# One ring of raw weight tiles for all stages, and a post-norm whose steps are tied to chunks

## The chip, the cores and the metric

The kernel runs on one core of one Trainium2 chip. The metric is the device time of one execution in microseconds (us), the median over the runs. Every time below is in us unless marked ns.

## The reference

The kernel computes two layers of a decoder trunk on 1024 tokens of width 1024, all in float32. Cut to what matters:

```python
for l in range(2):
    h = rms_norm(x, pre_mix_norm[l])
    z = h @ w_in[l]                     # conv columns, q, k, v of 4 heads
    u = silu(layer_norm(dwconv31(c_a * sigmoid(c_g))))
    o = (softmax(q1 k1^T) - lam * softmax(q2 k2^T)) v    # causal, rotary on part of q and k
    m = concat([u, rms_norm(o) * c]) @ w_out[l]
    x = x + rms_norm(m, post_mix_norm[l])
    h = rms_norm(x, pre_ffn_norm[l])
    g, val = split(dwconv3(h @ w_up[l]))                 # 2 x 2816 columns
    f = (gelu(g) * val) @ w_down[l]
    x = x + rms_norm(f, post_ffn_norm[l])
```

## The kernel before

Each layer is two stages, each with tile pools of its own in SBUF. The mixing stage holds both projections, the convolution and the attention. The feed-forward stage holds the up-projection (with the short convolution and the gate) and the down-projection.

Every matrix product is made to float32 accuracy from rounded parts. A weight block comes from memory as a "raw" tile. ScalarE (ACT) copies it to a rounded high part; VectorE (DVE) or GpSimd (POOL) subtracts to get the low part; TensorE (PE) then runs three matmuls for each pair of blocks. In the mixing stage this is the helper pair `load` (L443) and `split` (L458): raw tile `raw` of 512 columns in a ring of RAW = 3 in pool `mw`, parts in `whw`, `wlw`, `whq`, `wlq`. In the feed-forward stage it is `parts` (L1276), with the parts in `wo` (seven buffers) and, in the down-projection, `wp` (five buffers).

The mixing stage is ordered by a planner, `Flow`. It keeps a clock for each engine and emits instructions in the order in which its costs say they become ready. Its `Ring` objects mirror the numbers of buffers, RAW among them, so that another RAW gives another plan. It orders PE, DVE, ACT and POOL.

The up-projection uses a Strassen-like scheme of seven products for each pair of column tiles, written out as a list `seq` of slots; `prep` (L1396) splits one weight operand, seven slots ahead. Its raw weight tiles are 1024 columns wide (512 KB), in two tags, `rg` and `rv`, of two buffers each, in the stage's pool `fw_`. `next_raw` (L1379) starts one load; it is called four times ahead of the first slot and then after certain splits. The first eight columns named in EARLY run ahead as products "e1" and "e2".

The down-projection runs seven products j = 1, 2, 5, 3, 6, 7, 4, each over K2 = 11 chunks k (`run`, L1613). In each chunk it prepares the operands of the chunk that comes three later, and the last two or three chunks are a tail in which PE finishes one token tile after the other. After product 6 the first half of the tokens is complete but for a sum that the function `end6` makes; its post-norm, and in the first layer the next layer's pre-norm and transposes, are a generator for each of four token tiles, `post_steps(tt)`. A queue `bg` of the four is stepped two or three times in each chunk, so that two generators are under way together:

```python
def step(q):
    g = q.popleft()
    if next(g, None) is not None:
        q.insert(min(1, len(q)), g)
```

Each generator takes one tile `y` and one tile `xr`, both from rings of two. `end7` makes the other half's sum from the PSUM banks, `pa`, that product 4 goes on to accumulate in; `end4` is the second half's post-norm.

The order of the DMA queue (SP, shown as SPq) isn't written by hand: the framework places each load where it becomes ready by its own schedule, in any order of the program. A tile in a pool that is open for the whole program needs a free slot for that; a tile in a stage's pool needs in addition the pool to have opened, after what came before in that part of SBUF. `gvec` loads the norm gains into a ring of two in such a lasting pool: the calls that bear on this are L1603, near the end of the up-projection, and L1745, late in the down-projection, for the next layer.

Of the kernel before, what the change touches and what calls it, by code (L numbers as in the profile page):

```python
# [9 lines left out]
F32 = mybir.dt.float32  # L10
# [7 lines left out]
P = 128  # L18
# [3 lines left out]
HB = 512  # L22
# [33 lines left out]
E_BUFS = 5  # L56
LATE = 12
XR = 2
RAW = 3
AT_BUFS = 2  # L60
CB = ((9, 0, 1, 2), (0, 1, 2, 3))

# [151 lines left out]
def build(tc, ap, out):  # L214
# [7 lines left out]
    with ExitStack() as top:  # L222
# [9 lines left out]
        ptr = pool(top, "ptr", bufs=2, space=PSUM)  # L232
        pO = pool(top, "pO", bufs=1, space=PSUM)
        dr = pool(top, "dr", bufs=1, space=DRAM)

        def const(name, shape, dt=F32):
            return cst.tile(shape, dt, tag=name, name=name)
# [178 lines left out]
        for l in range(DEPTH):  # L416
            xres = xin if l == 0 else x2[l - 1]
            with ExitStack() as st:
# [24 lines left out]
                def load(key, src, n, tag, gate=None):  # L443

                    wi = yield from R[tag].get()
                    size, bufs = (768, 4) if tag == "q" else (1024, 2)
                    hi = mw.tile([P, size], F32R, tag=f"wh{tag}", name=f"wh{tag}", bufs=bufs)
                    lo = mw.tile([P, size], F32R, tag=f"wl{tag}", name=f"wl{tag}", bufs=bufs)
                    W[key] = hi, lo, wi
                    step = n if n <= HB else n // 2  # L450
                    for j in range(n // step):
                        ri = yield from R["raw"].get()
                        raw = mw.tile([P, HB], F32, tag="raw", name="raw", bufs=RAW)
                        s = slice(j * step, (j + 1) * step)
                        sy.dma_start(raw[:, :step], src[:, s])
                        fl.spawn(split(key, j, raw[:, :step], hi[:, s], lo[:, s], step, ri, gate), fl.now + W_LAT)
# [809 lines left out]
            with ExitStack() as st:  # L1266
# [36 lines left out]
                with ExitStack() as su:  # L1303
# [64 lines left out]
                    for tt in range(4):  # L1368
                        before[NORM_T[tt]] = tt
                        for step in range(4):  # L1370
# [2 lines left out]

                    raws, wsum, W = {}, {}, {}

                    loads = deque([("e", n, "gv"[q % 2], 0) for q, n in enumerate(early)]
                                  + [("m", n, "gv"[v], v) for n in range(NFT) for v in range(2)])

                    def next_raw():  # L1379
                        if loads:  # L1380
                            k, n, t, v = loads.popleft()
                            raw = fw_.tile([P, 1024], F32, tag="r" + t, name="raw", bufs=2)
                            sy.dma_start(raw, wu[2 * order[n] + v])
                            raws["gv"[v], (k, n)] = raw[:, 0:HB], raw[:, HB:1024]

# [10 lines left out]
                    def prep(j, n):  # L1396
                        g = raws["g", ("e" if j in ("e1", "e2") else "m", n)]
                        if j in (6, 5, 7, 3):
                            if j == 6:
                                wsums(n, 1, 2)  # L1400
                            elif j in (5, 7):
                                wsums(n, 3 if j == 5 else 4)
                            x = wsum[n][{6: 2, 5: 1, 7: 3, 3: 4}[j]]
                        elif j == 4:
                            x = raws["v", ("m", n)][1]
                        else:
                            x = g[j in (2, "e2")]
                        W[j, n] = parts(x, po)
                        if j in ("e2", 3, 4):
                            next_raw()  # L1410

                    for _ in range(4):
# [197 lines left out]
                with ExitStack() as sd:  # L1610
                    dn = pool(sd, f"dn{l}", bufs=1, reuse_waits="tile")

                    def run(j, ps, first, tail, ends):  # L1613

                        c0 = [x[0] for x in chunks].index(j)
                        cuts = [(k,) for k in range(K2 - tail)] + [tuple(range(K2 - tail, K2))]
                        for cut in cuts:
                            for k in cut:
                                c = c0 + k
                                for _ in range(1 + c % 2):  # L1620
                                    fetch()
                                for ahead, task in ((F_AHEAD, fetch_f), (P_AHEAD, prepare)):
                                    if c + ahead < len(chunks):
                                        task(c + ahead)
                                sum_w(c)
                                for _ in range(2 + (j == 7 and k % 2)):
                                    if bg:
                                        step(bg)
                            for tt in range(4):
                                ts = slice(tt * P, (tt + 1) * P)  # L1630
                                for k in cut:
                                    (ah, al), (wh, wl) = ops[c0 + k]
                                    for n, (x, y) in enumerate(((ah[:, ts], wh), (al[:, ts], wh), (ah[:, ts], wl))):
                                        pe.matmul(ps[tt], x, y, start=first and k + n == 0, stop=k == K2 - 1 and n == 2,  # L1634
                                                  skip_group_check=not first)
                                if cut[-1] == K2 - 1 and j == 4:
                                    ends(tt)
                        if j != 4:
                            for tt in range(4):
                                ends(tt)  # L1640

                    bg = deque()

                    def step(q):

                        g = q.popleft()
                        if next(g, None) is not None:
                            q.insert(min(1, len(q)), g)

                    def post_steps(tt):  # L1650

                        m0, s2 = m0s[tt]
                        ps1 = u2[tt]
                        y = xs.tile([P, YW], F32, tag="y", name="y", bufs=2)[:, 0:D]
                        xr = load_x(x1[l][tt])
                        se.activation(y[:, 0:HB], ps1, AF.Square, accum_out=s2[:, 1:2])
                        ve.tensor_tensor(y[:, HB:D], ps1, g_pf[:, HB:D], op=ALU.mult)
                        ss = xs.tile([P, 1], F32, tag="ss", name="ss", bufs=3)
                        ve.tensor_tensor(ss, s2[:, 0:1], s2[:, 1:2], op=ALU.add)
                        r = rstd_from_sum(ss, 1.0 / D)  # L1660
                        yield 1
                        ve.scalar_tensor_tensor(y[:, 0:HB], m0, r, xr[:, 0:HB], op0=ALU.mult, op1=ALU.add)  # L1662
                        ve.scalar_tensor_tensor(y[:, HB:D], y[:, HB:D], r, xr[:, HB:D], op0=ALU.mult, op1=ALU.add)  # L1663
                        sy.dma_start(out[tt * P:(tt + 1) * P, :] if last else x2[l][tt], y)
                        if last:
                            return
                        ss = xs.tile([P, 1], F32, tag="ss", name="ss", bufs=3)
                        se.activation(xr, y, AF.Square, accum_out=ss)
                        yield 1
                        r = rstd_from_sum(ss, 1.0 / D)  # L1670
                        yield 1
                        ve.scalar_tensor_tensor(xr, y, r, g_pre, op0=ALU.mult, op1=ALU.mult)
                        yield 1
                        yield 1
                        sl = slice(tt * P, (tt + 1) * P)
                        for gi in range(2):
                            pt = ptr.tile([P, 4, P], F32, tag="tr", name="pt")
                            for j in range(4):
                                pe.transpose(pt[:, j, :], xr[:, (gi * 4 + j) * P:(gi * 4 + j + 1) * P], ident)
                            se.activation(nhA[gi][:, 0, :, sl], pt, AF.Copy)  # L1680
                            yield 1
                            ve.tensor_tensor(nhA[gi][:, 1, :, sl], pt, f32(nhA[gi][:, 0, :, sl]), op=ALU.subtract)
                            yield 1

                    def keep(name):
                        return [dn.tile([P, HB], F32, tag=name, name=name, bufs=4) for _ in range(4)]
# [9 lines left out]
                    own = [dn.tile([P, HB], F32, tag="wb", name="wb", bufs=12) for _ in range(12)]  # L1696
                    spB = [t[:, j] for t in inB for j in range(8)]
                    B.update({"dn": dn, "12": spB[0:K2], "22": own[1:12], "21": B["A"][K2:16] + spB[K2:16] + own[0:1]})
                    pa = banks(0)
                    u2, vv = keep("u2"), keep("vv")  # L1700
                    for _ in range(5):
# [42 lines left out]
                    else:  # L1744
                        g_pre = gvec(l + 1, 0)  # L1745
                        nhA = alloc_h("hA")
                    bg.extend(post_steps(tt) for tt in range(4))
                    run(7, pa, False, DTAIL, end7)

                    def end_last(tt):  # L1750
                        nonlocal nhB
                        if tt == 0:
                            while bg:
                                step(bg)
                            manual.close()
                            if not last:
                                nhB = alloc_h("hB")
# [75 lines left out]
```

## Time and profile before

| | |
|---|---|
| time, median of 3 runs | 2364.84 |
| lowest and highest | 2364.63, 2525.17 |
| profiled execution | 2363.12 |
| its span, first to last instruction | 2361.0 |
| mean granted TensorE clock | 0.969 of full speed |
| weight data and all else moved by DMA | 295.39 MB |

The profile is of one execution. PE is matmuls, PEld weight loads, which overlap them; DVE, ACT, POOL and SP are the other engines. A row of the chain of waits says which line of the program waited for which, and how long. In the timeline a bracket gives the idle time of that engine ahead of the instruction and what ended it. L1634 are the matmuls of the down-projection, L1583 those of the up-projection, L495 those of the mixing stage; L1279 is ACT's half of a split, L1280 the subtraction. In the first layer the mixing stage takes the first 500, and the down-projection ends near 1190.

### The profile page before, as it was taken

Reading aid. Unit: us, or ns where it says so; the run is one execution under the profiler, and the core shown is the slowest. Engines: PE = TensorE matmul, PEld = TensorE weight load, DVE = VectorE, ACT = ScalarE, POOL = GpSimd, SP = SyncE. Lnnn points to the kernel's source line nnn. Section 1 sums busy time; section 2 is a strip of 40 time slices with the busy share of each in tenths; the row PEclk is TensorE's granted clock in tenths of the full one; section 3 lists DMA queues with packets and bytes.
Section 4 is the critical chain, followed back from the end, with each engine's and each line's share of the span. In section 5 each row is a group of like instructions: output and inputs, shape, how many; then the busy total and the mean of one; then the engine's idle time right before and its main releaser. Section 6 shows DMA issues by size and latency. Waiting matters only on the chain. (4 is left out here: it accounts for less than half of the span.)

```text
span 2361.0 us, 31535 instructions
## 1 busy us (share of the span) xinstructions
PE 2203.4 (93%) x10568; PEld 1837.9 (78%) x10568; DVE 1857.8 (79%) x3285; ACT 1131.9 (48%) x2458; POOL 827.4 (35%) x896
## 2 busy tenths in 40 slices
PE   6999997959999999999879999979699999999997
PEld 4998886748877878788659988867588778787886
DVE  6889989537888888777768899895478888887777
ACT  4445456535544544444534455565364444445443
POOL 3224312235454554201532233122345445542024
PEclk8999998979999999999979999989899999999999
DMA  4222323534333333933333133235443333348343
GB/s 145 69 63 90 85 80 111 188 137 161 107 125 118 123 130 114 321 110 93 126 114 81 52 89 90 75 112 196 144 143 107 125 128 111 132 138 310 101 151 108
DMA packets 140129, 295.39 MB, mean 125 GB/s; under 512 B 16832, under 2 KB 33984, under 8 KB 139456
## 3 DMA queue, kind: packets, MB, share of 16 engines
q1 hardware_dynamic: 139968, 293.39, 38.9%
q8 instruction: 83, 1.36, 0.2%
q14 instruction: 78, 0.64, 0.1%
HBM read 198.44 MB, written 78.12 MB: 117 GB/s over the span
## 5 line engine op out<-in xcount | busy, mean ns | idle before, releaser
L1634 PE MATMUL pd<-wp,wo 128*128 128x512 f32 x1776 | 409.8, 392 | 8.3 <-DVE wp L1280 4.9
L1634 PEld LDWEIGHTS pd<-wp,wo 128*128 128x128 f32 x1776 | 333.7, 189 | 81.2 <-DVE wp L1280 6.5
L1583 PE MATMUL py<-t,wo 128*128 128x512 f32 x1584 | 377.4, 391 | 4.5 <-DVE cg L1451 4.5
L1583 PEld LDWEIGHTS py<-t,wo 128*128 128x128 f32 x1584 | 296.6, 188 | 73.3 <-ACT wo L1279 7.7
L1280 POOL TENSOR_TENSOR wo<-ws,wo 128x512 fp32r<-128x512 f32 x176 | 252.8, 1448 | 283.0 <-ACT wo L1279 251.2
L1583 PE MATMUL px<-hA,wo 128*128 128x512 f32 x1056 | 262.6, 401 | 43.3 <-ACT wo L1279 42.1
L1583 PEld LDWEIGHTS px<-hA,wo 128*128 128x128 f32 x1056 | 200.3, 190 | 93.5 <-ACT wo L1279 43.0
L1280 POOL TENSOR_TENSOR wo<-raw,wo 128x512 fp32r<-128x512 f32 x132 | 176.7, 1343 | 146.3 <-ACT wo L1279 136.9
L1280 POOL TENSOR_TENSOR wo<-fa,wo 128x512 fp32r<-128x512 f32 x66 | 102.4, 1568 | 311.2 <-ACT wo L1279 287.0
L1279 ACT ACTIVATE wo<-ws 128x512 fp32r<-128x512 f32 x176 | 108.4, 626 | 135.3 <-PE py L1583 54.5
L1469 DVE SCALAR_TENSOR_TENSOR acc<-cg,fw,acc 128x512 f32<-128x512 f32 x176 | 132.6, 753 | 41.7 <-ACT acc L1457 38.0
L593 DVE SCALAR_TENSOR_TENSOR scr<-u,cw,scr 128x256 f32<-128x256 f32 (+2 forms) x288 | 159.7, 574 | 0.3
L495 PE MATMUL pq<-whq,hA 128*128 128x384 f32 x512 | 136.4, 348 | 5.9 <-ACT whq L459 5.9
L1457 ACT ACTIVATE acc<-cg,fb,fw 128x512 f32<-128x512 f32 x88 | 68.2, 775 | 147.8 <-DVE cg L1451 147.8
L495 PE MATMUL pq<-whq,hB 128*128 128x384 f32 x512 | 134.4, 343 | 0.0
L1583 PE MATMUL pz<-b,wo 128*128 128x512 f32 x528 | 131.1, 397 | 2.0 <-DVE cv L1451 2.0
L1583 PE MATMUL pz<-t,wo 128*128 128x512 f32 x528 | 130.5, 396 | 0.0
L848 ACT ACTIVATE e<-S,mxv 128x512 f32<-128x512 f32 (+2 forms) x192 | 109.7, 578 | 42.4 <-DVE mxv L843 30.9
L853 POOL TENSOR_TENSOR sm<-sm 128x1 f32<-128x1 f32 x64 | 29.5, 461 | 274.6 <-ACT e L848 274.6
L839 DVE TENSOR_REDUCE mxv<-S 128x1 f32<-128x512 f32 (+2 forms) x192 | 100.6, 548 | 28.3 <-PE S L823 26.2
L1583 PEld LDWEIGHTS pz<-b,wo 128*128 128x128 f32 x528 | 98.4, 188 | 28.2 <-issue 5.2
L1583 PEld LDWEIGHTS pz<-t,wo 128*128 128x128 f32 x528 | 99.0, 188 | 23.6
(279 smaller groups left out, 4985.3 us busy)
## 6 DMA issues: line engine op xcount, KB each, us to landing
raw<-in_wupd SPq DMA_DIRECT2D x104, 512.0 KB, 3.7
fa<-f SPq DMA_DIRECT2D x154, 256.0 KB, 2.7
f<-fs SPq DMA_DIRECT2D x88, 256.0 KB, 3.6
raw<-in_wmix SPq DMA_DIRECT2D x80, 256.0 KB, 2.9
f<-gg SPq DMA_DIRECT2D x66, 256.0 KB, 2.0
raw<-in_wmix SPq DMA_DIRECT2D x64, 192.0 KB, 2.5
qs<-sth SPq DMA_DIRECT2D x64, 128.0 KB, 2.8
os<-onT SPq DMA_DIRECT2D x16, 512.0 KB, 2.9
```

Source lines behind the costliest of these rows:

```text
L495: mm = pe.matmul(dst, a, b, start=first and k + j == 0, stop=final and k == n - 1 and j == 2)
L593: ve.scalar_tensor_tensor(dst, src, wk, dst, op0=ALU.mult, op1=ALU.add)
L839: ve.tensor_reduce(mv_[:, j:j + 1], S, axis=AX.X, op=ALU.max, negate=True)
L848: se.activation(e[:, c0:c0 + w], S, AF.Exp, bias=mv_[:, 0:1], accum_out=sm[:, j:j + 1])
L853: po.tensor_tensor(sm[:, 0:1], sm[:, 0:1], sm[:, 1:2], op=ALU.add)
L1279: se.activation(w[:, 0], raw, AF.Copy)
L1280: eng.tensor_tensor(w[:, 1], raw, f32(w[:, 0]), op=ALU.subtract)
L1457: se.activation(acc[n, v, hf], C[n][v][:, 2 + hf * HB:2 + hf * HB + HB], AF.Identity, bias=fb[:, mt:mt + 1], scale=fw[:, mt, 2:3])
L1469: ve.scalar_tensor_tensor(dst, c[:, j + hf * HB:j + hf * HB + HB], fw[:, mt, j:j + 1], a, op0=ALU.mult, op1=ALU.add)
L1583: pe.matmul(ps, x, y, start=first and k + j == 0, stop=k == 3 and j == 2, skip_group_check=not first)
L1634: pe.matmul(ps[tt], x, y, start=first and k + n == 0, stop=k == K2 - 1 and n == 2, skip_group_check=not first)
```

## The change

A pool `rw` is opened at the start of the program and stays open. The raw tiles of both stages come from it: one tag, RAW = 4 buffers of 1024 columns. The mixing stage's ring so grows from three to four, in the plan too, and the up-projection's two tags become one ring in the same order of loads. One of the calls of `next_raw` moves from behind the split for product 3 to behind that for product 7, one slot earlier in `seq`.

The queue `bg` becomes a list, and each generator advances by at most one step in a chunk: tile 0 from chunk 0 of product 7, tile 1 from chunk 3, tile 2 from chunk 6, tile 3 from chunk 8, and all in every chunk of product 4. The steps are cut anew: the square and the first product are a step of their own, and the last subtraction no longer has one.

```diff
-RAW = 3
+RAW = 4
+        rw = pool(top, "rw", bufs=1)
...
-                        raw = mw.tile([P, HB], F32, tag="raw", name="raw", bufs=RAW)
+                        raw = rw.tile([P, 1024], F32, tag="raw", name="raw", bufs=RAW)
...
-                    loads = deque([("e", n, "gv"[q % 2], 0) for q, n in enumerate(early)]
-                                  + [("m", n, "gv"[v], v) for n in range(NFT) for v in range(2)])
+                    loads = deque([("e", n, 0) for n in early] + [("m", n, v) for n in range(NFT) for v in range(2)])
...
-                            raw = fw_.tile([P, 1024], F32, tag="r" + t, name="raw", bufs=2)
+                            k, n, v = loads.popleft()
+                            raw = rw.tile([P, 1024], F32, tag="raw", name="raw", bufs=RAW)
...
-                        if j in ("e2", 3, 4):
+                        if j in ("e2", 7, 4):
                             next_raw()
...
-                                for _ in range(2 + (j == 7 and k % 2)):
-                                    if bg:
-                                        step(bg)
+                                for tt, q in enumerate((0, 3, 6, 8)):
+                                    if j == 7 and k >= q or j == 4:
+                                        next(bg[tt], None)
...
                         ve.tensor_tensor(y[:, HB:D], ps1, g_pf[:, HB:D], op=ALU.mult)
+                        yield 1
                         ss = xs.tile([P, 1], F32, tag="ss", name="ss", bufs=3)
...
                             ve.tensor_tensor(nhA[gi][:, 1, :, sl], pt, f32(nhA[gi][:, 0, :, sl]), op=ALU.subtract)
-                            yield 1
...
-                    bg.extend(post_steps(tt) for tt in range(4))
+                    bg = [post_steps(tt) for tt in range(4)]
                     run(7, pa, False, DTAIL, end7)
...
-                            while bg:
-                                step(bg)
+                            for g in bg:
+                                for _ in g:
+                                    pass
```

## Rows read from the trace of the kernel before

**Rows 1.** The page, part 1: busy time, share of the span, instructions.

```profile
...
PE 2203.4 (93%) x10568; PEld 1837.9 (78%) x10568; DVE 1857.8 (79%) x3285; ACT 1131.9 (48%) x2458; POOL 827.4 (35%) x896
```

**Rows 2.** TensorE's waits, whole span: us in total, times, longest us.

```profile
...
PE px L1583 <- ACT wo L1279: 42.1, 2, 23.1
...
PE pg L495 <- ACT whw L459: 9.3, 1, 9.3
...
PE pq L495 <- ACT whq L459: 5.9, 4, 4.1
...
PE pt L1679 <- DVE xr L1672: 5.2, 3, 2.1
```

**Rows 3.** Timeline, first layer's mixing end: start, us, engine, line [idle before].

```profile
...
508.15 0.58 ACT L1156 ACTIVATE pw<-pw 128x512 f32<-128x512 f32 x1 [4.51 <-DVE xn L1153]
...
512.40 0.18 ACT L1172 ACTIVATION_READ_ACCUMULATOR xn<-xe 128x1 f32 x1
...
514.80 0.33 SPq L246 DMA_DIRECT2D gb<-in_norms  x1
...
516.34 10.78 SPq L1383 DMA_DIRECT2D raw<-in_wupd  x6
520.99 0.63 ACT L1279 ACTIVATE wo<-raw 128x512 fp32r<-128x512 f32 x1 [8.40 <-DMA raw<-in_wupd]
...
521.67 0.79 PE L1583 MATMUL px<-hA,wo 128*128 128x512 f32 x1 [23.12 <-ACT wo L1279]
```

**Rows 4.** Timeline of VectorE, same stretch: the last split of a mixing weight.

```profile
...
483.00 0.69 DVE L465 TENSOR_TENSOR wlq<-raw,whq 128x512 fp32r<-128x512 f32 x1 [1.00 <-ACT whq L459]
```

**Rows 5.** The page, part 6: up-projection loads: KB, us to landing.

```profile
...
raw<-in_wupd SPq DMA_DIRECT2D x104, 512.0 KB, 3.7
```

**Rows 6.** Timeline, second layer's end of mixing.

```profile
...
1690.37 0.19 ACT L1172 ACTIVATION_READ_ACCUMULATOR xn<-xe 128x1 f32 x1
...
1695.55 0.80 PE L1583 MATMUL px<-hA,wo 128*128 128x512 f32 x1 [19.03 <-ACT wo L1279]
```

**Rows 7.** Timeline, the second layer's first product.

```profile
...
1197.85 0.63 ACT L391 ACTIVATE y<-s 128x512 f32<-128x512 f32 x1 [0.97 <-DVE nl L298]
...
1198.48 1.91 ACT L459 ACTIVATE whw<-raw 128x512 fp32r<-128x512 f32 x3
...
1199.15 0.80 PE L495 MATMUL pg<-hA,whw 128*128 128x512 f32 x1 [9.34 <-ACT whw L459]
```

**Rows 8.** Timeline, the second layer's first query weights.

```profile
...
1221.18 1.01 PE L495 MATMUL pq<-whq,hA 128*128 128x384 f32 x2 [4.14 <-ACT whq L459]
...
1228.38 1.00 ACT L459 ACTIVATE whq<-raw 128x384 fp32r<-128x384 f32 x2 [2.47 <-DMA raw<-in_wmix]
```

**Rows 9.** Timeline, first layer, products 7 and 4 of the down projection.

```profile
...
1128.37 1.12 PE L1679 MATMUL pt<-ident,xr 128*128 128x128 f32 x4 [2.15 <-DVE xr L1672]
...
1153.57 0.93 PE L1634 MATMUL pd<-wp,wo 128*128 128x512 f32 x3 [2.88 <-DVE vv L1722]
...
1163.71 0.63 PE L1679 MATMUL pt<-ident,xr 128*128 128x128 f32 x4 [1.59 <-DVE xr L1672]
```

**Rows 10.** Table by stretch: us, busy of each engine, granted clock, DMA.

```profile
...
1128.40:1131.00 2.60, 2.60 (x9) 2.21 (x10) 1.59 (x1) 1.48 (x3) 1.33 (x2) 0.50 0.51 131
...
521.70:526.50 4.80, 4.24 (x9) 3.06 (x10) 0.00 (x0) 3.34 (x6) 4.76 (x4) 0.50 0.36 146
```

**Rows 11.** Timeline, second layer, product 7 of the down projection.

```profile
...
2309.54 40.78 PE L1634 MATMUL pd<-wp,wo 128*128 128x512 f32 x178 [2.05 <-DVE wp L1280]
```

**Rows 12.** Tile xr, 1100 to 1190: ns min/median/max, first, last.

```profile
...
L1663 DVE SCALAR_TENSOR_TENSOR y<-y,rs,xr x4: 740/1260/1780, 1117.5 to 1147.1; 128x512 f32<-128x512 f32 x4
...
DMA to landing us min/median/max: 3.3/3.4/3.5
```

**Rows 13.** Table by stretch: the two stretches of attention.

```profile
...
200.00:400.00 200.00, 182.25 (x1063) 162.39 (x1062) 178.61 (x432) 111.44 (x330) 55.83 (x96) 0.95 0.31 92
...
1400.00:1600.00 200.00, 182.20 (x1063) 161.10 (x1062) 176.92 (x432) 109.01 (x322) 48.65 (x90) 0.95 0.31 92
```

More of the change, by code (lines that the diff above doesn't have):

```diff
@@ L1374, in build @@
                     raws, wsum, W = {}, {}, {}
-                    loads = deque([("e", n, "gv"[q % 2], 0) for q, n in enumerate(early)]
-                                  + [("m", n, "gv"[v], v) for n in range(NFT) for v in range(2)])
+                    loads = deque([("e", n, 0) for n in early] + [("m", n, v) for n in range(NFT) for v in range(2)])
                     def next_raw():
                         if loads:
-                            k, n, t, v = loads.popleft()
-                            raw = fw_.tile([P, 1024], F32, tag="r" + t, name="raw", bufs=2)
+                            k, n, v = loads.popleft()
+                            raw = rw.tile([P, 1024], F32, tag="raw", name="raw", bufs=RAW)
                             sy.dma_start(raw, wu[2 * order[n] + v])
@@ L1640, in run @@
                                 ends(tt)
[L1642 to L1648, printed above, removed]
                     def post_steps(tt):
@@ L1698, in build @@
                     B.update({"dn": dn, "12": spB[0:K2], "22": own[1:12], "21": B["A"][K2:16] + spB[K2:16] + own[0:1]})
+                    bg = None
                     pa = banks(0)
```

## The prediction

> **What bounds the kernel now.** I first read the busy times on the page: TensorE (PE) is busy for 2203.4 of the span of 2361.0, no other engine for more than 79% [rows 1]. The end is set by PE's work and by 158 us in which PE stands still, so the question for each part of the change is which of PE's pauses it shortens. I then read the chain of waits of PE, longest sum first. The largest is two pauses, 42.1 in all, in which the first matmul of the up-projection (L1583) waits for ACT's first split (L1279), once a layer. Far behind come 9.3 at the second layer's first product, 5.9 for the query weights behind it, and 5.2 in three pauses in which transposes of the next layer's input (L1679) wait for the post-norm's scaling (L1672) [rows 2]. The timeline shows what each pause hangs on. In the first layer, ACT ends its mixing work at 512.58; the DMA queue issues the load of a norm gain at 514.80 and only from 516.34 the raw up-projection weights; ACT splits the first at 520.99 and PE starts at 521.67 [rows 3]. The reader is to see that the weights come late because of their place in the queue: the gain at 514.80 is the second of two loads there, that of L1745, some 360 lines of program further on, for a gain that L1672 first wants 600 us later [rows 9]. It lies in a pool that is always open and goes as soon as its slot is free. The raw weights lie in a stage's pool, and go after the last of the mixing stage.
>
> **The up-projection's start.** The change puts the raw tiles into a pool of the first kind. The four slots are free when the last mixing weight is split, at 483.69 [rows 4]; a load lands in 3.7 [rows 5], four of them one after the other in at most 15. So all four are there by 499, 13 before ACT is done. What is late next is ACT itself: its order is written out, and its split follows its last mixing instruction. Its parts (`wo`) are still in the stage's pool, so I don't expect it to move ahead of that. PE then starts 0.68 after the split does, as now: 512.58 + 0.68 = 513.26 in place of 521.67, which is 8.4 [rows 3]. In the second layer ACT ends at 1690.56, so PE starts at 1691.24 in place of 1695.55, 4.3 [rows 6]. Sum 12.7. The half clock behind each pause stays: PE was granted 0.50, its level of 1.2 GHz, for the 4.8 after the pause of 23.12 [rows 3, 10], and it also was after a pause of only 2.15 [rows 9, 10], so a pause of 15 should cost the same again.
>
> **The other edits of the loads.** The up-projection's two tags of two become one ring of four in the same order of loads, alternating as before: nothing. Calling `next_raw` after product 7 in place of 3 issues one load one product earlier, twelve matmuls of 40.78 / 178 = 0.229 or 2.7 [rows 11]; two columns are already there, so it is hidden, and would cost nothing if it weren't. It moves past no load that PE waits for. The prefetched mixing weights of the second layer, four of 256 KB, lie in the queue among hundreds of loads of the first layer: nothing.
>
> **The second layer's start.** Here the pause doesn't hang on the load alone. ACT's first split at 1198.48 follows L391 of the last token tile at 1197.85 without a gap [rows 7], and the parts `whw` are in the mixing pool, which opens behind the same work. The 9.3 stays. Behind it, one raw tile more in the ring brings each later load one place forward. ACT waits 2.47 for a load at 1228.38; PE waits 4.14 at 1221.18 for a split that was planned late [rows 8]. No row shows the plan for a ring of four. I bound this by nothing and by the whole 5.9 of the query weights [rows 2], and take 3, because the pause of 4.14 is the plan's choice and not the load's, and may or may not go. The first layer's start waits for the input; I take nothing.
>
> **The post-norm.** In the first layer, transposes wait 5.2 in three pauses; one of 2.15 ends at 1128.37 and is followed by 2.60 at half clock, and one of 1.59 ends at 1163.71 [rows 2, 9, 10]. Two generators started together reach their scaling together, with the transposes close behind. In the fixed steps the scaling (fifth step) and the first transposes (seventh) are two chunks apart and one generator does a heavy step at a time, so the first two pauses, 5.2 - 1.6 = 3.6, go, and with them half of 2.60, 1.3: 4.9. The third, in product 4, I keep: tile 3 starts only in chunk 8 and scales in product 4's chunk 1.
>
> The edit adds a wait. Tile 2 starts in chunk 6, while tile 0's `xr` is read until its second transposes in chunk 7; with two buffers, its load waits for them, and tile 3's, asked for in chunk 8, for tile 1's in chunk 10. The wait stands on the DMA queue, with the loads of activations five chunks ahead behind it; then on DVE, two steps later, with the splits of later chunks behind it on DVE and ACT. The load lands 3.3 to 3.5 after its issue [rows 12]. For tile 2 the splits are three chunks ahead, which covers it. For tile 3, PE's transposes stand just ahead of the tail of chunks 9 and 10. Two sets of four take some 0.7 (the one at 1163.71 shows 0.63, its end beside what follows [rows 9]), the tail's 24 matmuls 5.5 [rows 11], so PE wants the sum in the bank at 6.2. The load lands at 0.7 + 3.4 = 4.1; the two steps L1662 and L1663 take 0.74 and between 0.74 and 1.78 [rows 12]; `end7`'s first sum, 0.69 like other DVE steps of that size [rows 4], ends at 6.3 to 7.3. That leaves 0.1 to 1.1. For each of three further token tiles DVE needs two such steps, 1.4, and PE three matmuls, 0.7: another 2.1. Together 2.2 to 3.2, much like the 2.88 that PE waits there for L1722 now [rows 9]. So this pause stays too, for another reason.
>
> The steps of L1663 range from 740 to 1780 ns [rows 12]; the long ones run beside a subtraction on POOL. The Trainium skill (SBUF — State Buffer, Who interferes with whom) says that a DVE instruction with two SBUF inputs and a GpSimd instruction that reads SBUF exclude one another, and the later waits for the whole of the other. Fixed steps put every heavy step into a chunk that has a subtraction on POOL, so by that rule tile 3's two steps ahead of `end7` would both take 1.78 and the total be about 1 us higher than mine.
>
> In the second layer the post-norm ends with the store; there is no transpose, and a tile is free again early. PE's one pause of 2.05 in product 7 [rows 11] comes from four post-norms in the first four chunks; spread over eleven, it goes: 2.05.
>
> **The sum.** 12.7 + 3 + 4.9 + 2.05 = 22.7 against the profiled execution's 2363.1: 2340.4. That execution lies 1.7 below the median of 2364.84, or 0.07%, so I give 2341 on the median's scale.
>
> **The rivals.** First, ACT's split doesn't wait for the end of the mixing work. Once the weights are there early, the framework could place it into ACT's gap of 4.51 ahead of 508.15 [rows 3]; PE would start at 503.64 + 0.68 = 504.3, a further 9.0, and the second layer's stage repeats the same order: 18 in all, 2323. Moved ahead of the whole tail it would remove what is left of both pauses, 14.7 each (23.12 - 8.4 and 19.03 - 4.3 [rows 3, 6]), and pass 2%. Against it: the order is by hand, and the parts' pool opens last. Chance 0.1, a third of it beyond 2%.
>
> Second, the change doesn't do what it says: the loads keep their place in the queue, because the queue's order comes from the framework's own times. The 12.7 is then lost, and 2354 is left. Against it speaks the gain that goes early [rows 3]. Chance 0.12.
>
> Third, slower: a ring of four gives another plan for both mixing stages. The place is attention, where PE stands for 17.8 of 200 in the first layer and 17.8 in the second, at a mean clock of 0.95 [rows 13]. A plan that puts splits ahead of softmax steps on ACT and DVE lengthens these. It decides from 22.7, when the two stretches lose two thirds of what they lose now again; if all of it, 35.6, the time is 2341 + 35.6 = 2377. Against it: the planner already takes a split as it comes due, and the number of splits is the same. Chance 0.12.
>
> **How the numbers follow.** My forecast, with its own bounds, has 0.66: the terms' low ends (no gain at the second layer's start, a post-norm that gains only what the second layer shows) give 12.7 + 2.05 and 2349, the high ends (5.9; all of the first layer's pauses and the half clock, 5.2 + 2.9 + 1.3) give 30 and 2334. The range has to reach to 2323 on the one side and into the third rival's lower half on the other: 2322 to 2362. It leaves out a third of the first rival and two thirds of the third, with a little for what I haven't seen. About 2%, or 47 us, is what I take a measurement of this kernel to tell from no change. Faster than that needs more than twice my sum, which only the far end of the first rival gives: 0.04. Slower needs a plan that loses over 70 in mixing: 0.02. Within: 0.94.
>
> **What would show it.** In the changed profile, the first raw up-projection loads should be issued near 485 and stand ahead of the stores of L1169; PE's wait for ACT there should be about 14.7 in each layer, with ACT's first split directly behind L1172. The 9.3 at the second layer's start should stand, still behind L391. In product 7 of the first layer no transpose should wait over 1, while DVE waits for a load of `xr` in chunks 8 and 10, and PE still some 3 for L1722. Wrong would be a first split that still waits for a DMA, a wait of the up-projection under 10, or an attention stretch with a busy PE that differs by over 5 from 182.

## Result, and the profile after

The changed kernel takes 2341.52 us (median of 2336.54, 2342.35, 2340.70, 2342.45), the kernel before, run beside it, 2364.84 (of 2364.84, 2364.63, 2367.01): a ratio of 0.9894 with a 95% interval of 0.9875 to 0.9914. Two executions at a lower clock count in no figure here, 2525.17 of the kernel before and 3131.99 of the experiment with the loads alone (the one of that kernel that was profiled). The forecast was 2341, within a range of 2322 to 2362. The number came out, its terms did not. The profiled execution is the fastest of the four, so its stages add up to 26.6 less than before, where the medians differ by 23.3.

The table is read from PE's timeline, by the first and last matmul of each stage's line (L495 before and L496 after, L1583, L1634); a stage that follows another without a pause counts from the other's end. The last 10.7 are the same in both.

| us | before | after | forecast's gain | gain |
|---|---|---|---|---|
| up to the first mixing product | 25.54 | 26.35 | 0 | -0.8 |
| mixing, layer 1 | 473.01 | 471.60 | 0 | 1.4 |
| pause, then up-projection, layer 1 | 23.12 + 439.52 | 0 + 447.41 | 8.4 | 15.2 |
| down, layer 1 | 228.62 | 230.95 | 4.9 | -2.3 |
| pause at the second layer's start | 9.34 | 9.41 | 0 | -0.1 |
| mixing, layer 2 | 477.37 | 478.05 | 3 | -0.7 |
| pause, then up-projection, layer 2 | 19.03 + 439.62 | 0 + 446.29 | 4.3 | 12.4 |
| down, layer 2 | 215.15 | 213.66 | 2.05 | 1.5 |

PE's busy time after, from the page's first part, against [rows 1]:

```profile
PE 2205.1 (94%) x10568; PEld 1841.9 (79%) x10568; DVE 1863.9 (80%) x3287; ACT 1126.9 (48%) x2458; POOL 829.9 (36%) x894
```

PE does the same work; what changed are its pauses. The chain of waits of PE after (us in total, times, longest), against [rows 2]:

```profile
PE px L1583 <- ACT ea L1436: 14.9, 2, 7.4
...
PE pg L496 <- ACT whw L460: 9.4, 1, 9.4
PE pd L1634 <- DVE vv L1715: 8.0, 4, 7.1
...
PE pq L496 <- ACT whq L460: 3.6, 1, 3.6
...
PE pt L1672 <- DVE hA L1675: 3.0, 2, 2.2
...
PE pt L1672 <- DVE ss L1652: 0.3, 1, 0.3
```

The first line is to be read with care: it is not the old wait of 42.1 shortened. The releaser was ACT's split of the weights; now it is `e_copy` (L1436), by which ACT takes the first early product out of its PSUM bank, so that the second can be added to it there. The timeline of the first layer's mixing end, against [rows 3]:

```profile
478.72 14.12 SPq L1383 DMA_DIRECT2D raw<-in_wupd  x7
482.32 0.63 ACT L1280 ACTIVATE wo<-raw 128x512 fp32r<-128x512 f32 x1 [3.48 <-DMA raw<-in_wupd]
484.25 2.45 ACT L1280 ACTIVATE wo<-raw 128x512 fp32r<-128x512 f32 x4 [1.30 <-DMA raw<-in_wupd]
487.34 1.15 ACT L1280 ACTIVATE wo<-raw 128x512 fp32r<-128x512 f32 x2 [0.64 <-DMA raw<-in_wupd]
497.79 5.75 PE L1583 MATMUL px<-hA,wo 128*128 128x512 f32 x24
498.93 3.24 SPq L1170 DMA_DIRECT2D x<-xe  x3
504.05 1.07 PE L1331 MATMUL pt<-ident,xn 128*128 128x128 f32 x8 [0.51 <-DVE ss L350]
507.57 0.58 ACT L1157 ACTIVATE pw<-pw 128x512 f32<-128x512 f32 x1 [4.50 <-DVE xn L1154]
510.87 1.06 ACT L1173 ACTIVATE xn<-xe 128x1024 f32<-128x1024 f32 x1 [2.61 <-DVE xe L1168]
511.93 0.58 ACT L1436 ACTIVATE ea<-px 128x512 f32<-128x512 f32 x1
512.55 7.68 PE L1583 MATMUL px<-hA,wo 128*128 128x512 f32 x21 [7.44 <-ACT ea L1436]
```

The raw loads are issued from 478.72 on, ahead of the stores (L1170). Seven splits, as many as there are `wo` tiles, stand on ACT ahead of the mixing tail, so PE runs from its last mixing product into the up-projection without a pause. It does two products and eight transposes and then meets what had been hidden: `e_copy` stands behind the tail's last square at 510.87. The second layer repeats this, with 7.44 too: of the 42.1 that the two pauses took before, 14.9 come back.

In product 7 the steps on the way to L1715 (L1722 before), against [rows 9]:

```profile
1116.76 0.60 PE L1672 MATMUL pt<-ident,xr 128*128 128x128 f32 x4
1118.81 3.43 SPq L1551 DMA_DIRECT2D fa<-f  x2
1122.30 0.42 SPq L242 DMA_DIRECT2D xr<-x  x1
1126.32 0.75 DVE L1655 SCALAR_TENSOR_TENSOR y<-m0d,rs,xr 128x512 f32<-128x512 f32 x1 [1.86 <-DMA xr<-x]
1127.82 1.06 ACT L1661 ACTIVATE xr<-y 128x1024 f32<-128x1024 f32 x1 [6.27 <-DVE y L1656]
1128.13 0.42 SPq L242 DMA_DIRECT2D xr<-x  x1
1130.01 0.61 ACT L1280 ACTIVATE wp<-wb 128x512 fp32r<-128x512 f32 x1
1130.65 1.34 DVE L1281 TENSOR_TENSOR wp<-wb,wp 128x512 fp32r<-128x512 f32 x1 [2.32 <-ACT wp L1280]
1133.46 2.18 DVE L1665 SCALAR_TENSOR_TENSOR xr<-y,rs,gb 128x1024 f32<-128x1024 f32 x1
1135.56 0.74 DVE L1655 SCALAR_TENSOR_TENSOR y<-m0d,rs,xr 128x512 f32<-128x512 f32 x1
1136.23 0.74 DVE L1656 SCALAR_TENSOR_TENSOR y<-y,rs,xr 128x512 f32<-128x512 f32 x1
1136.89 0.68 DVE L1715 TENSOR_TENSOR vv<-pd,vv 128x512 f32<-128x512 f32 x1
1137.71 5.37 PE L1634 MATMUL pd<-wp,wo 128*128 128x512 f32 x12 [7.05 <-DVE vv L1715]
...
1151.82 0.66 PE L1672 MATMUL pt<-ident,xr 128*128 128x128 f32 x4 [2.22 <-DVE hA L1675]
```

PE ends product 7 at 1130.66. Tile 0's last transposes, which free the place of tile 2's `xr`, end at 1117.36. Tile 2's load goes only at 1122.30: it stands in the queue right behind two loads of activations (L1551), which waited for POOL's subtractions. DVE stands until 1126.32; ACT's square of that tile follows at 1127.82, ACT's splits for later chunks behind the square, DVE's half of them at 1130.65; then come tile 2's scaling and tile 3's sums, and only at 1136.89 the addition that PE waits for.

### The profile page after: what moved, and what is told of

It is laid out like the page before. It is cut to its first block, busy times and chain, and to the rows that moved or that the text cites. A ratio compares the mean times of both kernels' runs of the same rounds, so it can differ in the third digit from the quotient of the medians.

```text
span 2334.4 us, 31508 instructions
## 1 busy us (share of the span) xinstructions
PE 2205.1 (94%) x10568; PEld 1841.9 (79%) x10568; DVE 1863.9 (80%) x3287; ACT 1126.9 (48%) x2458; POOL 829.9 (36%) x894
## 5 line engine op out<-in xcount | busy, mean ns | idle before, releaser
L1634 PE MATMUL pd<-wp,wo 128*128 128x512 f32 x1776 | 410.6, 393 | 10.8 <-DVE vv L1715 8.0
L1634 PEld LDWEIGHTS pd<-wp,wo 128*128 128x128 f32 x1776 | 334.7, 189 | 83.4 <-issue 7.4
L1583 PE MATMUL py<-t,wo 128*128 128x512 f32 x1584 | 377.4, 391 | 4.7 <-DVE cg L1451 4.7
L1583 PEld LDWEIGHTS py<-t,wo 128*128 128x128 f32 x1584 | 296.7, 188 | 73.5 <-ACT wo L1280 8.0
L1583 PE MATMUL px<-hA,wo 128*128 128x512 f32 x1056 | 261.7, 400 | 14.9 <-ACT ea L1436 14.9
L1583 PEld LDWEIGHTS px<-hA,wo 128*128 128x128 f32 x1056 | 200.6, 191 | 64.0 <-ACT ea L1436 15.4
L496 PE MATMUL pq<-whq,hA 128*128 128x384 f32 x512 | 134.8, 344 | 3.6 <-ACT whq L460 3.6
L496 PE MATMUL pq<-whq,hB 128*128 128x384 f32 x512 | 134.2, 343 | 0.0
L1583 PE MATMUL pz<-b,wo 128*128 128x512 f32 x528 | 131.0, 396 | 2.0 <-DVE cv L1451 2.0
L1583 PE MATMUL pz<-t,wo 128*128 128x512 f32 x528 | 130.5, 396 | 0.0
L1583 PEld LDWEIGHTS pz<-b,wo 128*128 128x128 f32 x528 | 98.3, 188 | 28.2 <-issue 5.1
L1583 PEld LDWEIGHTS pz<-t,wo 128*128 128x128 f32 x528 | 99.0, 188 | 23.6
```

The costliest lines, as they stand in the source:

```text
L496: mm = pe.matmul(dst, a, b, start=first and k + j == 0, stop=final and k == n - 1 and j == 2)
L1583: pe.matmul(ps, x, y, start=first and k + j == 0, stop=k == 3 and j == 2, skip_group_check=not first)
```

## The experiments

Line numbers move by a few between kernels. Each ratio is to the kernel before on the same chip, with its 95% interval.

**The loads alone.** The changed kernel with the old `step(bg)` and its calls, the old yields, and all edits of the loads.

> The changed kernel's loads (one lasting ring of four, its plan, the load order of the up-projection) with the post-norm steps of the kernel before. Theory A, from the stages of the changed kernel's trace: the loads alone make the gain, 15.2 and 12.4 us between the mixing's last matmul and the up-projection's last in the two layers, and the fixed steps of the post-norm cost 2.3 us in the first layer and give 1.5 in the second. So about 2366 - 27 = 2339 us, the down stage of the first layer back near 228.8 us, and PE waits for L1722 (the adds behind product 7) near 2.9 instead of 7.1. Rival B, the forecast's sum: the loads give 12.7 and some 3 at the layer's start, so 2350.

Measured: 2337.12, 0.9883 (0.9868 to 0.9898). This is theory A; the forecast's 2350 is excluded. The whole gain is the loads'. The stages can be read from the run with three buffers below, which has the old post-norm too: its pause behind product 7 is 2.88, as before.

**The post-norm alone.** The kernel before, with

```
-  for _ in range(2 + (j == 7 and k % 2)):
-      if bg:
-          step(bg)
+  for tt, q in enumerate((0, 3, 6, 8)):
+      if j == 7 and k >= q or j == 4:
+          next(bg[tt], None)
```

and the yields as changed.

> The kernel before with only the fixed steps of the post-norm. Theory A: 2.3 us lost in the first layer's down stage and 1.5 won in the second's, so 2366.8 us, with the pause behind product 7 near 7 us. Rival B, the forecast: 4.9 and 2.05 won, so 2359.

Measured: 2364.72, 0.9998 (0.9989 to 1.0006), which is between 2.6 faster and 1.4 slower than before. My 7 are excluded. Its waits show where they went:

```profile
PE px L1583 <- ACT wo L1279: 42.8, 2, 23.5
...
PE pd L1634 <- DVE vv L1715: 7.6, 4, 6.7
```

The old wait of the up-projection is back with the old loads, and the pause behind product 7 (2.88 before) is 6.7 without any change of the loads. The other waits of the post-norm are those of the changed kernel.

**The forecast's order.** The changed kernel with ACT's splits kept behind the tail:

```
-  se.activation(xn, x, AF.Square, accum_out=ss)
+  mixend.append(se.activation(xn, x, AF.Square, accum_out=ss))
...
-  se.activation(w[:, 0], raw, AF.Copy)
+  i = se.activation(w[:, 0], raw, AF.Copy)
+  if mixend:
+      after(i, mixend[-1])
```

> The changed kernel with one more order: the up-projection's splits on ACT stay behind the last square of the mixing stage's tail, as the forecast assumed; the raw loads stay early. Theory A: that the seven splits run ahead of that tail is what gives more than the forecast said; held back, PE waits some 14.7 us ahead of its first up-projection product in each layer, the 7.4 us before the e2 products go, and the time is about 2341.5 + 14.9 = 2356. Rival B: the early raw loads are enough and the order on ACT doesn't matter; 2341.

Measured: 2350.98, 0.9935 (0.9922 to 0.9949). The timeline at the first start, and the chain of waits:

```profile
511.36 1.06 ACT L1175 ACTIVATE xn<-xe 128x1024 f32<-128x1024 f32 x1 [2.60 <-issue]
...
512.41 3.73 ACT L1282 ACTIVATE wo<-raw 128x512 fp32r<-128x512 f32 x7
513.08 0.79 PE L1587 MATMUL px<-hA,wo 128*128 128x512 f32 x1 [14.63 <-ACT wo L1282]
```

```profile
PE px L1587 <- ACT wo L1282: 29.2, 2, 14.6
```

This is the kernel that I forecast: pauses of 14.63 and 14.61, where I gave 14.7 each, so 8.5 and 4.4 less than before, where I gave 8.4 and 4.3. The raw loads go at 479.22 here too. So early loads alone give 12.9, and that the splits run ahead of the tail gives the rest: the pauses of 14.6 become copies' waits of 7.4. From the last mixing product to the last of the up-projection it takes 455.33 and 454.17, against 447.41 and 446.29: 15.8 more. The median is only 9.5 above the changed kernel's, because the changed kernel's profiled execution lies 5.0 below its median, and this one near its own.

**The plan alone.** The kernel before with `RAW = 4`, which there is only the mixing stage's own ring.

> The kernel before with four buffers instead of three in the mixing stage's own raw ring (its plan is made anew for four); nothing else. Theory A: the plan changes the attention stretches by no more than 1 us and the waits for the query weights by 2 to 3; 2363 to 2366 us. Rival, the forecast's slower case: the new plan costs both mixing stages, up to 2377.

Measured: 2366.96, 1.0005 (0.9995 to 1.0014), so by its interval the new plan gives at most 1.2 and costs at most 3.3. The two attention stretches of the changed kernel, against [rows 13] (busy PE, PEld, DVE, ACT and POOL, then the granted clock):

```profile
200.00:400.00 200.00, 182.64 (x1030) 160.93 (x1029) 178.21 (x422) 106.88 (x315) 54.23 (x90) 0.91 0.29 84
1400.00:1600.00 200.00, 182.64 (x1024) 158.40 (x1023) 172.70 (x415) 110.67 (x320) 45.37 (x85) 0.91 0.34 99
```

PE's busy times differ by 0.4 from before, but that sign, which I had set, doesn't decide it: at a clock of 0.91 in place of 0.95, PE got through 1030 matmuls in place of 1063 in the first layer's stretch. What speaks against the third rival is the time: it needed 22.7, and the first mixing stage as a whole is 1.4 shorter than before. A small cost stays open. The second mixing stage took 477.4, 477.6 and 478.0 in the three traces with a ring of three, and 478.1 to 483.4 in nine with a ring of four; that is one execution of each kernel.

**Three buffers in the lasting ring.** The loads as changed, `RAW = 3`, and the old post-norm.

> The kernel with the lasting ring and the new load order, but three buffers, the plan of the mixing stage as before, and the old post-norm steps. Theory A: what counts is that the buffers outlive the mixing stage; three raws hold what the first four splits need, so the up-projection starts as in the changed kernel: 2338 to 2342 us. Rival B: the fourth buffer makes a part of the gain (the splits of the third pair come late); 2345 to 2350.

Measured: 2337.29, 0.9880 (0.9866 to 0.9893), as the loads alone with four. Its up-projections take 446.41 and 446.26 from the last mixing product, as the changed kernel's 447.41 and 446.29. Its timeline:

```profile
483.80 0.63 ACT L1280 ACTIVATE wo<-raw 128x512 fp32r<-128x512 f32 x1 [1.13 <-DMA raw<-in_wupd]
486.34 2.25 ACT L1280 ACTIVATE wo<-raw 128x512 fp32r<-128x512 f32 x4 [1.92 <-DMA raw<-in_wupd]
493.05 1.15 ACT L1280 ACTIVATE wo<-raw 128x512 fp32r<-128x512 f32 x2 [4.45 <-DMA raw<-in_wupd]
...
498.18 5.75 PE L1583 MATMUL px<-hA,wo 128*128 128x512 f32 x24
```

The last pair of splits comes 5.7 later than with four buffers and still ahead of PE's start. What counts is that the ring outlives the stage; the fourth buffer gives nothing that can be measured.

**What the pause behind product 7 is made of.** Two kernels move steps behind it. In both, tile 3's post-norm reads the factor of the second half's last tile, which `end7` has put into its place by then. So they compute something else, and serve to read the waits; the number and kind of the instructions are the same. First, tile 3 begun in product 4: `(0, 3, 6, K2)`.

> The changed kernel with tile 3's post-norm begun in product 4 instead of in chunk 8 of product 7. Theory A: of the 7.1 us behind product 7, tile 3 has 2.5 to 3.5 (its two adds of 0.74, its product of 0.68, its sums on DVE and its square on ACT, all ahead of L1715); tile 2's wait for its xr load (1.9) and the chain behind it stay. Pause 3.6 to 4.6, time about 2338.5. Rival B: the pause is the xr load's; it stays near 7, time 2341.

Measured: 2330.29, 0.9848 (0.9832 to 0.9864). The pause is 4.8: tile 3 has 2.3 of it. The time is 11 below the changed kernel's, where I expected some 3. The profiled executions are only 4.0 apart, with 4.5 of gain in the first layer's down stage and 1.8 in the second's, against 2.7 of loss in mixing; the changed kernel's lies 5.0 below its median and this one 2.0 above, and no trace shows the rest. Second, no step in the tail's two chunks either:

```
-  if j == 7 and k >= q or j == 4:
+  if j == 7 and q <= k < K2 - DTAIL or j == 4:
```

> The changed kernel with no post-norm step in the last two chunks of product 7, and tile 3 begun in product 4. Theory A: the 7.1 us that PE waits behind product 7 in the first layer are DVE's and ACT's steps of tiles 2 and 3 that stand ahead of L1715 in the hand order; with them behind it the pause falls to 0 to 1.5 us, some 2 us come back as waits of transposes in product 4, and the time is about 2341 - 4 = 2337. Rival B: the steps are only put off, and as much is lost in product 4 or at the next layer's start; 2341.

Measured: 2329.57, 0.9850 (0.9835 to 0.9864). The pause is 4.69, hardly less, so my 0 to 1.5 fell: with tile 2's scaling out of the way DVE still waits 1.50 for `xr` and 2.31 for ACT's split behind the square, as in the changed kernel (1.86 and 2.32). The second layer's down stage is 1.8 shorter here too.

With tile 3's own factor kept (one of the second half's four goes into a dead `u2` tile):

> As the run that held the steps back from the last two chunks of product 7, but tile 3 keeps its own factor (its buffer stays taken until product 4; the first of the second half's factors goes into a dead u2 tile). Theory A: the same order of work, so the pause behind product 7 is 4.7 us and the time 2330. Rival B: the kept buffer makes DVE or ACT wait in product 4; 2335 or more.

Measured: 2331.83, 0.9849 (0.9833 to 0.9866), with a pause of 5.1 and 3.2 at a transpose in product 4. Then tile 2 one chunk later as well, with its factor kept in the same way, so that its wait for `xr` comes behind product 7:

> As hold_fixed, with tile 2 begun one chunk later (7), so that its adds, which wait for its xr load, come behind product 7 too. Theory A: of the 4.7 us, the 1.5 of DVE's wait for xr and the 2.3 of its wait for ACT's splits behind tile 2's square go; the pause falls to 1 us or less and the time to 2326 or 2327. Rival B: the pause moves to the transposes of tiles 2 and 3 in product 4; 2330.

Measured: 2331.35, 0.9851 (0.9833 to 0.9870). The chain of waits and the timeline:

```profile
PE pt L1673 <- DVE xr L1666: 4.3, 1, 4.3
...
PE pd L1635 <- DVE vv L1716: 1.3, 3, 0.7
```

```profile
1131.14 0.96 PE L1635 MATMUL pd<-wp,wo 128*128 128x512 f32 x3 [0.74 <-DVE vv L1716]
...
1146.40 1.09 PE L1673 MATMUL pt<-ident,xr 128*128 128x128 f32 x4 [4.34 <-DVE xr L1666]
```

Each theory holds by half. The pause behind product 7 goes (0.74), which shows that it was tile 2's chain from `xr` on; 4.34 of it appears at tile 2's transposes in product 4, and the time stays.

**The copy's pause.** The changed kernel with a third `e1` product ahead of the first `e2`, on the bank that attention's output has left:

```
-  seq = [... for q in range(0, len(early), 2) for j in ("e1", "e2") for n in early[q:q + 2]]
+  seq = [... for q in (early[:3], early[3:5], early[5:7], early[7:]) for j in ("e1", "e2") for n in q]
...
-  px[n] = (pmm.tile(...) if j == "e1" else
+  px[n] = (pmm.tile(...) if j == "e1" and n != early[2] else
```

> The changed kernel with a third e1 product (on the bank that the attention's output has left) ahead of the first e2 product. Theory A: PE waits 7.4 us in each layer there because ACT copies the first e1 result only behind the last square of the mixing's tail; 2.9 us more work ahead of the wait takes 2.9 us of it, pauses near 4.5, time about 2341 - 5.9 = 2335. Rival B: the copies on ACT, now three in a row, push the wait on by as much; 2341.

Measured: 2336.27, 0.9868 (0.9848 to 0.9888).

```profile
504.18 3.05 PE L1583 MATMUL px<-hA,wo 128*128 128x512 f32 x12
511.86 8.43 PE L1583 MATMUL px<-hA,wo 128*128 128x512 f32 x24 [4.64 <-ACT ea L1436]
```

The pause shrinks by the product put ahead of it, 7.44 to 4.64, as expected; a further wait of 0.74 comes later. From the last mixing product to the last of the up-projection it takes 1.9 and 1.3 less than in the changed kernel. The time agrees with that, but its interval overlaps the changed kernel's. Putting the copies ahead of the tail's last square on ACT was not run.

**Both together.** `hold_later` with the third `e1` product.

> hold_later with the third e1 product ahead of the first e2. Theory A: the two pauses lie in different stages, so the gains add: 2326.5 - 5.6 = 2321. Rival B: with the steps of the up-projection's first groups moved, other waits take 2 to 3 us of it; 2324.

Measured: 2332.20, 0.9857 (0.9843 to 0.9872). PE's pauses in it are those of its two parts (4.65 in each layer ahead of the copies, 0.73 behind product 7, 4.34 in product 4), so the pauses add in the trace, but the time is 8 to 11 above what either theory gave. The time of the three kernels with a kept factor can't be told apart. All three intervals are clear of the changed kernel's; `hold_fixed` has the lowest ratio.

## Why the prediction was right, and where it wasn't

**The up-projection's start: right in its mechanism, wrong in one step.** The loads move as forecast, from 516.34 [rows 3] to 478.72, where I gave some 485; so the second rival, that they keep their place, is refuted. The step that failed is "its split follows its last mixing instruction": ACT's splits stand ahead of the tail. The first rival, at a chance of 0.1, described this and took all of 14.7 for its stronger form. Its price was wrong too: PE's next wait, for the copy behind the same tail, takes 7.4 back. The run with the forecast's order gives my numbers (14.63, 14.61), so the working from [rows 3, 6] holds for the case that I chose. By the bound I had set myself, an up-projection wait under 10, that step is refuted.

Why does the split go ahead here and not at the second layer's start? There the four raw tiles come early too:

```profile
904.59 0.33 SPq L456 DMA_DIRECT2D raw<-in_wmix  x1
...
985.60 0.33 SPq L456 DMA_DIRECT2D raw<-in_wmix  x1
...
1170.96 0.64 ACT L392 ACTIVATE y<-s 128x512 f32<-128x512 f32 x1 [7.57 <-DVE s L1720]
...
1185.05 2.17 ACT L460 ACTIVATE whw<-raw 128x512 fp32r<-128x512 f32 x4
1185.72 0.79 PE L496 MATMUL pg<-hA,whw 128*128 128x512 f32 x1 [9.41 <-ACT whw L460]
```

ACT is idle for 7.57 ahead of 1170.96, with the raw tiles there for 185 us, and splits at 1185.05. The `whw` tiles take the place of tiles that the down stage still uses, while the `wo` tiles take that of attention tiles long dead. So a split needs both its input early and its output's place free. This contrast is argued from the trace and the tiles' places; no run moved the `whw` tiles, and the framework's own order at the two borders is a rival that no run excludes. That pause stayed at 9.4, as forecast.

**The half clock: nothing gained, as forecast.** Behind the copy's pause PE runs at half clock as long as it did behind the longer one [rows 10]:

```profile
505.20:512.60 7.40, 0.05 (x1) 0.05 (x1) 3.77 (x7) 2.42 (x6) 1.15 (x3) 0.68 0.35 127
512.60:517.60 5.00, 5.00 (x12) 3.98 (x13) 4.53 (x6) 2.40 (x5) 4.25 (x3) 0.50 0.48 142
```

A pause of 7.4 is followed by 5.0 at 0.50, one of 23.1 was by 4.8.

**The second layer's start: 3 forecast, none seen.** PE's wait for the query weights' split by ACT fell from 5.9 to 3.6, that for POOL's part rose, and the second mixing stage takes 0.7 longer. The plan alone gives nothing either. My low end, zero, was the value, or a small loss.

**The post-norm, first layer: 4.9 forecast, nothing gained.** The stage is 2.3 longer in the table, but with the old steps it took 228.62, 231.16 and 231.14 (before, the plan alone, three buffers), at a mean clock of 0.99, 0.97 and 0.97, so that loss isn't shown. PE's idle time in it is: 10.3 to 10.4 in these three, 12.1 and 11.8 with the fixed steps (the changed kernel, the post-norm alone). The first two waits of transposes go from 3.60 to 1.06, so 2.5 of 3.6. The third grew from 1.59 to 2.22. The half clock's 1.3 didn't come, for the pause of 7.05 has its own: a clock of 0.52 in the 5.3 behind it. The step that failed is "for tile 2 the splits are three chunks ahead, which covers it". I followed tile 3's load to `end7`; it lands in time, and DVE takes tile 3's sums at 1135.56 without waiting for it. Tile 2's load, two chunks earlier, sets the time. I had put the loads of activations behind it in the queue; it stood behind two of them and went 4.9 after its place was free. DVE's order, then ACT's square, then ACT's splits, then DVE again carry its delay on. That tile 3's own steps have only 2.3 of it, and that the pause leaves product 7 when tile 2's steps do, is shown by the three runs.

The Trainium skill (SBUF — State Buffer, Who interferes with whom) says that a DVE step with two SBUF inputs and a GpSimd step that reads SBUF exclude one another; by that rule the prediction had tile 3's two steps at 1.78 each. They took 0.74, with POOL idle at the time. The rule agrees with tile 2's scaling, which began 0.16 after a subtraction on POOL and took 2.18, where a step of that size and kind took 1.28 at 502.62 (L1180), beside no more than 128x1 steps on POOL.

**The post-norm, second layer: 2.05 forecast, 1.5 gained.** The pause of 2.05 became two of 0.36. Here the stage shows it as well: 214.9 to 216.7 in three traces with the old steps, 213.6 to 213.7 in four with the fixed ones.

So 2341 was met by an excess of 14.9 at the two starts, against a lack of 7.8 in the post-norms and 3.2 in mixing and its starts. The profiled execution lies 3.9 below my sum, the median 0.5 above my 2341. (That figure had a slip of 1: the sum of 2340.4 is 2342.1 on the median's scale.) That errors of opposite sign cancelled so far is chance.

## What to carry to other kernels

When a stage's inputs are made to arrive early, ask for each instruction behind them whether its output's place is free as well, which the two starts suggest and no run here tested. If it is, the next stage's work can move into the gaps of this one's tail, and the next wait in line is for whatever of it shares an engine with that tail. Follow a late load through every engine whose written order it enters, not only to the instruction that reads it; the wait that ended last was two engines away, and the load itself was late behind others in its queue. A sum that comes out right says little of its terms until each is measured alone: here the loads gave twice what they should have and the post-norm nothing.

## What the runs showed of the hardware

PE's work in a mixing stage does not take the same time in each execution. In the second layer, in which every kernel here does the same matmuls (in two orders, by the plan), it was busy for 449.2 before, 449.4 after, 451.8 with the post-norm alone and 454.3 with the plan alone, at a mean granted clock of 0.95, 0.95, 0.94 and 0.94. In the up-projection behind it, it was busy for 435.8, 435.3, 435.9 and 435.4. Of the changed kernel's order alone, nine traces show 449.4 to 454.3. A spread of 5 is as much as most effects studied here, and is why the runs of the post-norm are read by their pauses.
